# The third value group by seven block products of half its columns, and another order for the last two rows of output tiles

## The chip, the cores and the metric

The kernel runs on one core of one Trainium2 chip. The metric is the device time of one execution in microseconds (us), the median of several runs. A core has five engines that work beside each other, each through its own queue in order: TensorE (PE in the rows; its weight loads are PEld), VectorE (DVE), ScalarE (ACT), GpSimd (POOL) and SyncE (SP), which issues transfers. ACT issues transfers too, in its own queue; those rows carry the name ACTq, as SP's carry SPq.

## The reference, cut to what matters

The kernel is one block of an encoder: a normalised input, one wide projection, three mixers, gates, an output projection and a normalised residual. The change touches the projection of the values of the dilated attention, and the last lines.

```python
h = rms_norm(x, g_pre[layer])                       # 1024 tokens x 1024
a_qkv, bq, ... = jnp.split(h @ w_in[layer], split_at, axis=-1)
a_qkv = a_qkv.reshape(b, s, 3, n_groups * A_HEADS, HEAD_DIM)
av = a_qkv[:, :, 2]                                 # values: three groups of 8 heads x 64 = 512 columns
...
out = merged @ w_out[layer]
x = x + rms_norm(out, g_post[layer])                # 1024 rows, the last tiles of 128 rows end the kernel
```

So one group of values is a product of 1024 tokens by 1024 (contracted) by 512 columns.

## The kernel before

All operands of the big products are kept as a sum of two fp32r parts, high and low. A product of two such operands takes three passes on TensorE: high by high, low by high, high by low. `split` (L104) makes the parts: ACT copies the source into the high part (L105), then DVE subtracts it from the source into the low part (L106).

The values are computed with the tokens as the stationary operand (128 by 128) and the weights as the moving one. Two of the three groups are done together by a block scheme with seven products in place of eight (`PRODUCTS`, L889: A11 by B11, A12 by B21, S2 by T2, S3 by T3, S4 by B22, S1 by T1, A22 by T4). The A and S are blocks of the weights and their sums, the B blocks of the tokens, and the T differences of token blocks that lie in DRAM (`tsd`) in fp32. Each product contracts 512 rows (4 steps k) and gives 512 tokens (4 tiles j) by 512 columns, so a step is 4 x 3 = 12 matmuls, and this first part has 28 steps. The third group (`VG[0]`) then goes the plain way: 2 halves of the tokens by 8 steps k by 4 tiles by 3 passes, 192 matmuls of 512 columns. Both are one loop over `steps_v` (L1088 to L1148), whose matmuls are L1101.

From L886 on the order on ACT, DVE, POOL and SP is the order in which the code is written (`manual_schedule`); TensorE's is so throughout. In each step of the loop the code writes the matmuls first, then the reading of one finished PSUM bank (`left`, `v_evac` L960), then the splits for the step two later (`split_at` L922), sums of weights (`sum_at` L942), the scaled copies with their transfers to DRAM (`v_store` L947: an ACT copy and a transfer that ACT issues), the loads of token differences (`blocks_at` L913), and `operand` (L978), an unrelated job for a later stage in eight rounds of three parts: loads, two DVE instructions, a store. Between the plain steps of the third group it also loads and splits the token differences again, for the keys (`kt_load`, `kt_split`, L1002 and L1006), and prepares the first weights of the keys (`k_load`, `k_sum`, `k_own`). The keys follow (L1165 on): six groups of seven products of 12 matmuls of 512 columns, whose matmuls are in `passes` (L125). Their first product needs the two parts that `k_own(0)` makes.

At the end the output projection runs as seven products too (`z_prod`, L2010). Its last bank, of row tile 7, is done in two halves of 256 columns (L2102 to L2114): each half is added up, squared on ACT with a sum, and weighed; `row(6)` (L2003), which adds row tile 6 to the input and sends it out, stands between the two halves.

Of the kernel before, what the change touches and what calls it, by code (L numbers as in the profile page):

```python
# [8 lines left out]
F32 = mybir.dt.float32  # L9
# [6 lines left out]
S = 1024  # L16
# [34 lines left out]
def block(ctx: ExitStack, tc: tile.TileContext, x, xT, memT, cst, msk, bcst, tabA, gpost,  # L51
# [832 lines left out]

    phase_psum("ps_v", s1=6)
# [4 lines left out]
    SB, TB_, v_rest = {}, {}, {}  # L890
    for k, t in enumerate(ready.pop(len(queue))):
        SB[0, k] = t
    vpp, vp = pool("vp")
    vbp, vb = pool("vb")
# [115 lines left out]
    kt_all = [(nm, k) for nm in ("T2", "T3", "T1", "T4") for k in range(4)]  # L1010
# [79 lines left out]
    for n, (i, e, k) in enumerate(steps_v):  # L1090
        if k == 0:
            now = v_banks()
        for j in range(4):
            if i is None:
                t = slice(e * 512 + j * 128, e * 512 + j * 128 + 128)
                (bh, bl), w, end = (hh[k][:, t], hl[k][:, t]), v_rest[k][0], 7
            else:
                (bh, bl), w, end = tokens_at(i, k, j), SB[i, k], 3
            wh_, wl_ = parts_of(w)
            for q, (a, b) in enumerate(((bh, wh_), (bl, wh_), (bh, wl_))):  # L1100
                PE.matmul(now[j], a, b, start=k == 0 and q == 0, stop=k == end and q == 2)  # L1101
        behind = left.pop(0)() if left else []
        m = n + 2
        if m < CLASSIC:
            split_at(*divmod(m, 4))
        elif m < CLASSIC + 8:
            split(*parts_of(v_rest[m - CLASSIC][0]), v_rest[m - CLASSIC][1])
# [5 lines left out]
        m = n + 5  # L1113
        if m < CLASSIC:
            blocks_at(*divmod(m, 4))
        elif m < CLASSIC + 8 and m % 2 == 0:
            raw = wp.tile([P, 1024], F32, name="wr", bufs=WR)
            nc.sync.dma_start(raw.rearrange("p (k f) -> p k f", k=2), wv[VG[0], :, m - CLASSIC:m - CLASSIC + 2])
            for z in range(2):
                v_rest[m - CLASSIC + z] = (wslot(z) if m < CLASSIC + 4 else slot(), raw[:, half[z]])  # L1120
# [4 lines left out]
        if n == CLASSIC + 4:  # L1125
            close(vbp)
            tpp, tp = pool("tp", "right")
            SF = [tp.tile([P, 512], F32, name=f"sf{j}") for j in range(4)]
        m = n - CLASSIC - 4
        if m >= 0:  # L1130
            for z in kt_all[2 * m:2 * m + 2] if m < 4 else kt_all[m + 4:m + 5]:
                kt_load(*z)
            for z in kt_all[2 * m - 6:2 * m - 4] if 3 <= m < 7 else kt_all[m + 1:m + 2] if 7 <= m < 11 else ():
                kt_split(*z)
            if m == 6:
                k_load(0, 0)
                k_load(0, 1)
            elif m == 10:
                k_own(0)
            elif m == 11:  # L1140
                k_sum(0, 1)
                k_sum(0, 2)
        if k == end:
            for j in range(4):
                if i is None:
                    left.append(lambda b=now[j], T=4 * e + j: [lambda: v_store(vr(), VG[0], T, b)])
                else:
                    left.append(lambda i=i, j=j, b=now[j]: v_evac(i, j, b))  # L1148
# [5 lines left out]
    close(vpp)  # L1154
# [10 lines left out]
    for n in range(6):  # L1165
        for i, (an, bn) in enumerate(PRODUCTS):
# [34 lines left out]
            if n == 0 and i < 4:  # L1201
                kt_split(*kt_all[12 + i])
# [800 lines left out]
    def row(T):  # L2003
# [241 lines left out]
```

## Time and profile before

| | us |
|---|---|
| median of 3 runs (1418.89 to 1419.91) | 1419.02 |
| the profiled execution | 1420.1 |
| its span, first to last instruction | 1418.3 |
| PE busy in the span | 1393.4 (98%) |
| DVE busy | 1040.7 (73%) |
| ACT busy | 670.6 (47%) |
| POOL busy | 505.1 (36%) |

A row of a timeline gives the start, the duration, the engine, the line, the operation, the tile that is written and those that are read, and, in brackets, how long the engine stood idle before it and what released it. "x24" means several alike in a row. A row of a table by stage gives the stretch, its length, the busy time of PE, PEld, DVE, ACT and POOL with the count of instructions, the clock that was granted to TensorE as a share of the full one, the share of the DMA engines' time, and GB/s. The profiled execution took 1.8 us more than its span, and 1.1 us more than the median.

### The profile page before, as it was taken

Reading aid. Unit: us, or ns where it says so; the run is one execution under the profiler, and the core shown is the slowest. Engines: PE = TensorE matmul, PEld = TensorE weight load, DVE = VectorE, ACT = ScalarE, POOL = GpSimd, SP = SyncE. Lnnn points to the kernel's source line nnn. Section 1 sums busy time; section 2 is a strip of 40 time slices with the busy share of each in tenths; the row PEclk is TensorE's granted clock in tenths of the full one; section 3 lists DMA queues with packets and bytes.
Section 4 is the critical chain, followed back from the end, with each engine's and each line's share of the span. In section 5 each row is a group of like instructions: output and inputs, shape, how many; then the busy total and the mean of one; then the engine's idle time right before and its main releaser. Section 6 shows DMA issues by size and latency. Waiting matters only on the chain.

```text
span 1418.3 us, 21284 instructions
## 1 busy us (share of the span) xinstructions
PE 1393.4 (98%) x7496; PEld 1120.2 (79%) x7496; DVE 1040.7 (73%) x1830; ACT 670.6 (47%) x1425; POOL 505.1 (36%) x390
## 2 busy tenths in 40 slices
PE   7999999999999999999999999999999999999997
PEld 7899986656666888888888878787888888888886
DVE  7768677767773695688885777765888788677977
ACT  6544365665555445322146676656543434222232
POOL 0416703766666000432153353520433331034303
PEclk9999999999999999999999999999999999999999
DMA  6356532322210779544543554555353543856255
GB/s 238 108 166 220 182 119 71 112 82 79 75 57 23 260 225 298 162 166 178 193 131 106 129 162 116 140 140 182 106 150 126 178 171 124 321 217 212 93 199 178
DMA packets 122059, 219.67 MB, mean 155 GB/s; under 512 B 25504, under 2 KB 56032, under 8 KB 121952
## 3 DMA queue, kind: packets, MB, share of 16 engines
q1 hardware_dynamic: 95744, 187.60, 41.1%
q10 hardware_dynamic: 26208, 30.71, 6.1%
q8 instruction: 59, 0.97, 0.3%
q14 instruction: 48, 0.39, 0.1%
HBM read 152.88 MB, written 65.37 MB: 154 GB/s over the span
## 4 chain that ended last, share of the span: by engine, by line
PE 78%; DVE 6%; DMA 5%; ACT 5%; issue 3%; POOL 2%; SPq 1%; DVEq 0%; POOLq 0%; ACTq 0%
PE s L125 23%; PE sc L125 9%; PE d L143 6%; PE d L145 6%; PE d L147 6%; PE ov L803 4%; PE s L2019 3%; PE s L1101 3%; PE s L1385 2%; PE tr L1441 2%; PE s L788 2%; PE s L787 2%; PE tr L769 2%; DMA vrt<-rld 2%; PE d L544 2%
## 5 line engine op out<-in xcount | busy, mean ns | idle before, releaser
L143 PE MATMUL d<-hh,wh 128*128 128x512 f32 x480 | 194.9, 406 | 1.7 <-DVE fth L228 1.7
L145 PE MATMUL d<-hl,wh 128*128 128x512 f32 x480 | 194.1, 404 | 0.0
L147 PE MATMUL d<-hh,wl 128*128 128x512 f32 x480 | 190.7, 397 | 0.0
L794 POOL TENSOR_TENSOR bl<-bl,bp 128x512 f32<-128x512 f32 x96 | 130.7, 1362 | 54.4 <-ACT bp L790 49.0
L105 ACT ACTIVATE wh<-wr 128x512 fp32r<-128x512 f32 (+1 forms) x91 | 69.6, 772 | 133.0 <-PE sc L125 78.7
L125 PE MATMUL sc<-hh,wh 128*128 128x512 f32 x384 | 118.4, 389 | 0.0
L106 DVE TENSOR_TENSOR wl<-wr,wh 128x512 fp32r<-128x512 f32 (+1 forms) x63 | 78.9, 1265 | 50.6 <-ACT wh L105 50.6
L143 PEld LDWEIGHTS d<-hh,wh 128*128 128x128 f32 x480 | 90.3, 188 | 27.1 <-issue 6.3
L147 PEld LDWEIGHTS d<-hh,wl 128*128 128x128 f32 x480 | 90.5, 189 | 21.1 <-issue 4.7
L1398 ACT ACTIVATE pra<-pra,sts 128x192 f32<-128x192 f32 (+2 forms) x192 | 84.3, 442 | 47.9 <-DVE sts L1397 47.4
L145 PEld LDWEIGHTS d<-hl,wh 128*128 128x128 f32 x480 | 90.5, 189 | 19.2 <-issue 4.7
L790 ACT ACTIVATE bp<-s 128x512 f32<-128x512 f32 x128 | 75.7, 595 | 43.3 <-PE s L788 42.3
L770 DVE TENSOR_REDUCE bn<-tr 128x1 f32<-128x512 f32 x128 | 84.8, 683 | 12.7 <-PE tr L769 11.3
L106 DVE TENSOR_TENSOR ch<-sf,ch 128x512 fp32r<-128x512 f32 x68 | 55.9, 823 | 40.5 <-ACT ch L105 40.4
L125 PEld LDWEIGHTS sc<-hh,wh 128*128 128x128 f32 x384 | 72.1, 188 | 15.1
L105 ACT ACTIVATE ch<-sf 128x512 fp32r<-128x512 f32 x68 | 41.6, 628 | 89.3 <-PE s L125 46.4
L1249 DVE SCALAR_TENSOR_TENSOR t2a<-d,tab 32x512 f32<-32x512 f32 x96 | 66.0, 687 | 22.4 <-PE d L147 20.7
L1925 POOL TENSOR_TENSOR acc<-acc,th 128x1024 f32<-128x1024 f32 x15 | 41.3, 2756 | 109.9 <-DVE th L1924 109.9
L1039 POOL TENSOR_TENSOR sf<-wr 128x512 f32<-128x512 f32 x12 | 19.0, 1580 | 168.7 <-DMA wr<-in_wu 111.1
L1708 POOL TENSOR_TENSOR sf<-wr 128x512 f32<-128x512 f32 x22 | 28.8, 1329 | 130.4 <-DVE ch L106 81.7
L125 PE MATMUL sc<-hl,wh 128*128 128x512 f32 x192 | 74.7, 389 | 0.0
L1253 POOL TENSOR_TENSOR aq<-t1a,t2a 128x512 f32<-128x512 f32 x24 | 44.5, 1858 | 82.1 <-DVE t1a L1252 82.1
(444 smaller groups left out, 3773.9 us busy)
## 6 DMA issues: line engine op xcount, KB each, us to landing
wr<-in_wu SPq DMA_DIRECT2D x64, 512.0 KB
kd<-kr ACTq DMA_DIRECT2D x48, 256.0 KB
th<-thd SPq DMA_DIRECT2D x24, 512.0 KB
thd<-rs ACTq DMA_DIRECT2D x44, 256.0 KB
g2d<-fth SPq DMA_DIRECT2D x24, 256.0 KB
wos<-os SPq DMA_DIRECT2D x12, 512.0 KB
kraw<-kd SPq DMA_DIRECT2D x12, 512.0 KB
kswp<-kd SPq DMA_DIRECT2D x48, 128.0 KB
```

The lines of the kernel that those rows point to most:

```text
L105: A.activation(dst_h, src, AF.Copy)
L106: V.tensor_tensor(dst_l, src, dst_h.bitcast(F32), op=OP.subtract)
L125: PE.matmul(out_ps, a, b, start=i == 0, stop=i == n - 1)
L143: PE.matmul(dst, wh[:, k, :], hh[k][:, t], start=k == 0, stop=False)
L145: PE.matmul(dst, wh[:, k, :], hl[k][:, t], start=False, stop=False)
L147: PE.matmul(dst, wl[:, k, :], hh[k][:, t], start=False, stop=k == 7)
L770: fp["last"] = V.tensor_reduce(st[i]["n"][:, j, c:c + 1], s, axis=AX.X, op=OP.min)
L790: A.activation(pp, s, AF.Exp, scale=-1.0)
L794: G.tensor_tensor(lsum[i % 2], lsum[i % 2], pp, op=OP.add)
L803: PE.matmul(o[e * 64:e * 64 + 64], VS[:, kt, kv], d.pop(kt), start=kt < 2, stop=kt >= NT - 2)
L1249: V.scalar_tensor_tensor(t2[i], p[j], -0.125, tab[1][j, t], op0=OP.mult, op1=OP.mult)
L1398: A.activation(src, src, AF.Exp, scale=-1.0, bias=bias, accum_out=sts[:, h, 1, T:T + 1])
```

## The change

The first part of the loop keeps its 28 steps; `operand` starts two steps earlier in it, and four transfers of weights for the third group are issued in its step 16. The third group then is a second loop of 28 steps over the same seven products, with half of its 512 columns as the one block and half as the other: a step is 12 matmuls of 256 columns (L1207), two token tiles share a PSUM bank, and the token differences T2, T3, T1, T4 are loaded and split within this loop and kept for the keys. What ACT, DVE, POOL and SP do beside each step is a table (`SIDE`). In the keys the four splits of T4 are gone. The pools `vb` and `vp` change places, since `vp` is closed first now.

The third group's results are scaled and stored by `v3_out`: per bank two ACT copies of 256 columns, each with a transfer of its own.

```diff
-    CLASSIC = 28
-    steps_v = [(i, 0, k) for i in range(7) for k in range(4)] + [(None, e, k) for e in range(2) for k in range(8)]
+    def v3_sum(nm, a, b, op, t=None):
+        V3[nm] = V3[a] if t is None else t
+        V.tensor_tensor(V3[nm], V3[a], V3[b], op=op)
+
+    def v3_split(nm):
+        h, l = wslot(0), wslot(1)
+        split(h, l, V3[nm])
...
+    def v3_out(u, t, b, r):
+        for z in range(2):
+            T = 4 * t + 2 * b + z
+            x = r[:, half_cols[z]]
+            A.activation(x, x, AF.Copy, scale=rcol[:, T:T + 1])
+            nc.scalar.dma_start(vdr[VG[0], 2 * u:2 * u + 2, T * 128:T * 128 + 128].rearrange("p t f -> t p f"),
+                                x.rearrange("t (p f) -> t p f", p=2))
...
+        if nm == "A11":
+            return [lambda: A.activation(v3v[b], ps_, AF.Copy)]
+        if nm == "A12":
+            r = add(r3(), v3v[b])
+            return [lambda: v3_out(0, 0, b, r)]
+        if nm == "S1":
+            x, y = add(r3(), v3y[b]), add(v3v[b], v3v[b])
+            return [lambda: v3_out(1, 1, b, x), lambda: v3_out(0, 1, b, y)]
+        if nm == "A22":
+            y = add(v3y[b], v3y[b])
+            return [lambda: v3_out(1, 0, b, y)]
+        add((v3y if nm == "S3" else v3v)[b], v3v[b])
...
         for stage in (2, 1, 0):
-            r, at = divmod(n - 6 - (0, 2, 3)[stage], 3)
+            r, at = divmod(n - 4 - (0, 2, 3)[stage], 3)
             if at == 0 and 0 <= r < 8:
                 operand(r, stage)
...
+        elif n == 24:
+            v3_split("A11")
+        elif n == 25:
+            v3_sum("S3", "A11", "A21", OP.subtract, V3["A21"])
+        elif n == 26:
+            v3_split("A12")
...
+    SIDE = {0: [lambda: operand(7, 2)], 2: [second], 3: [lambda: [kt_load("T3", k) for k in range(4)]], 4: [lambda: v3_split("S2")],
+            5: more(("T2", 0)), 6: more(("T2", 1), ("T2", 2)),
...
+            9: [lambda: v3_split("S3"), lambda: v3_sum("S4", "A12", "S2", OP.subtract)],
+            10: more(("T3", 0)) + [lambda: [kt_load("T4", k) for k in range(4)]],
+            11: more(("T3", 1)), 12: more(("T3", 2)) + [lambda: k_load(0, 0)], 13: more(("T3", 3)) + [lambda: v3_split("S4")],
...
+            24: more(("T4", 3)), 25: [lambda: k_own(0)], 26: [lambda: k_sum(0, 1)], 27: [lambda: k_sum(0, 2)]}
+    for n in range(28):
...
+        for _ in range(2 if n < 2 else 1):
+            for f in left.pop(0)() if left else []:
+                f()
...
+        for f in SIDE.get(n, ()):
+            f()
...
-            if n == 0 and i < 4:
-                kt_split(*kt_all[12 + i])
...
-        if h == 0:
-            row(6)
+        if h:
+            row(6, (lo,))
+        else:
+            V.tensor_tensor(c11[3][:, e], vs[3][:, e], gp[:, e], op=OP.mult)
         V.scalar_tensor_tensor(r, q[:, 2 * h:2 * h + 1], 1.0 / D, r, op0=OP.mult, op1=OP.add)
-        V.tensor_tensor(c11[3][:, e], vs[3][:, e], gp[:, e], op=OP.mult)
+    V.tensor_tensor(c11[3][:, e], vs[3][:, e], gp[:, e], op=OP.mult)
+    row(6, (hi,))
```

Three places show what this makes of the queues. The first is ACT in the changed kernel, where the third of the seven products runs and the fourth is prepared: r3 are the sums of the second product, vdr the values in DRAM, wh the high part of S3, and kT3 the token differences T3.

```order
L105 ACTIVATE kT23_5727<-kT23_5727 128x512
L1108 ACTIVATE r3_5843<-r3_5843,rcol_79 128x256
L1109 DMA vdr_110<-r3_5843 128x2x128
L1108 ACTIVATE r3_5843<-r3_5843,rcol_79 128x256
L1109 DMA vdr_110<-r3_5843 128x2x128
L1108 ACTIVATE r3_5861<-r3_5861,rcol_79 128x256
L1109 DMA vdr_110<-r3_5861 128x2x128
L1108 ACTIVATE r3_5861<-r3_5861,rcol_79 128x256
L1109 DMA vdr_110<-r3_5861 128x2x128
L105 ACTIVATE wh_5867<-wr_5382 128x1024
L105 ACTIVATE kT30_5743<-kT30_5743 128x512
```

The split of S3 stands behind four scaled copies with four transfers; nothing of this was there before.

The second place is ACT ahead of the keys. In the kernel before, wh is what `k_own(0)` makes for the first key product, and the four stores behind it are those of the last plain half:

```order
L105 ACTIVATE kT12_5874<-kT12_5874 128x512
L105 ACTIVATE kT13_5899<-kT13_5899 128x512
L105 ACTIVATE wh_5951<-wr_5880 128x1024
L948 ACTIVATE vr_5971<-s1_5813,rcol_79 128x512
L949 DMA vdr_110<-vr_5971 128x4x128
L948 ACTIVATE vr_5974<-s1_5814,rcol_79 128x512
L949 DMA vdr_110<-vr_5974 128x4x128
```

In the changed kernel, from the last split of T4 on, with v3v1 a sum that is stored in place:

```order
L105 ACTIVATE kT43_5892<-kT43_5892 128x512
L1108 ACTIVATE r3_6138<-r3_6138,rcol_79 128x256
L1109 DMA vdr_110<-r3_6138 128x2x128
L1108 ACTIVATE r3_6138<-r3_6138,rcol_79 128x256
L1109 DMA vdr_110<-r3_6138 128x2x128
L1108 ACTIVATE v3v1_5716<-v3v1_5716,rcol_79 128x256
L1109 DMA vdr_110<-v3v1_5716 128x2x128
L1108 ACTIVATE v3v1_5716<-v3v1_5716,rcol_79 128x256
L1109 DMA vdr_110<-v3v1_5716 128x2x128
L105 ACTIVATE wh_6149<-wr_5925 128x1024
```

`k_own(0)` has moved behind these four stores, and four like them (r3 and v3v0) stand ahead of the split of T4.

The third place is DVE at the end of the program, where cv3 and cp3 belong to row tile 7, fss7 is its sum of squares, and xt with fss6 is row tile 6. Before:

```order
L2105 TENSOR_TENSOR cv3_12946<-s1_13496,cv3_12946 128x256
L2007 SCALAR_TENSOR_TENSOR xt_13380<-cp2_12941,fss6_12960,xt_13380 128x512
L2007 SCALAR_TENSOR_TENSOR xt_13380<-acc2_12155,fss6_12960,xt_13380 128x512
L2109 SCALAR_TENSOR_TENSOR fss7_12961<-fss7_12961 128x1
L2110 TENSOR_TENSOR cp3_12942<-cv3_12946,rb_78 128x256
L2105 TENSOR_TENSOR cv3_12946<-s1_13496,cv3_12946 128x256
L2109 SCALAR_TENSOR_TENSOR fss7_12961<-fss7_12961 128x1
```

And in the changed kernel:

```order
L2179 TENSOR_TENSOR cv3_13144<-s1_13694,cv3_13144 128x256
L2184 TENSOR_TENSOR cp3_13140<-cv3_13144,rb_78 128x256
L2185 SCALAR_TENSOR_TENSOR fss7_13159<-fss7_13159 128x1
L2179 TENSOR_TENSOR cv3_13144<-s1_13694,cv3_13144 128x256
L2080 SCALAR_TENSOR_TENSOR xt_13578<-cp2_13139,fss6_13158,xt_13578 128x512
L2185 SCALAR_TENSOR_TENSOR fss7_13159<-fss7_13159 128x1
L2186 TENSOR_TENSOR cp3_13140<-cv3_13144,rb_78 128x256
L2080 SCALAR_TENSOR_TENSOR xt_13578<-acc2_12353,fss6_13158,xt_13578 128x512
```

The second half of row tile 7 is summed ahead of both halves of row tile 6, whose halves leave as two transfers in place of one.

More of the change, by code (lines that the diff above doesn't have):

```diff
@@ L1008, in kt_split @@
         split(h, l, l.bitcast(F32))
-    kt_all = [(nm, k) for nm in ("T2", "T3", "T1", "T4") for k in range(4)]
     KR = {}
@@ L1112, in block @@
             f()
[L1113 to L1120, printed above, removed]
+        if n < 23:
+            blocks_at(*divmod(n + 5, 4))
@@ L1126, in block @@
             close(vbp)
+            v3p, v3 = pool("v3")
             tpp, tp = pool("tp", "right")
+            v3v, v3y = [[v3.tile([P, 512], F32, name=f"v3{x}{b}") for b in range(2)] for x in "vy"]
+        elif n == 5:
             SF = [tp.tile([P, 512], F32, name=f"sf{j}") for j in range(4)]
[L1129 to L1148, printed above, removed]
+        for f in SIDE.get(n, ()):
+            f()
+        if k == 3:
+            left += [lambda i=i, b=b, z=now[b]: v3_evac(i, b, z) for b in range(2)]
     while left:
@@ L1153, in block @@
             g()
-    close(vpp)
+    close(v3p)
     tbp, tb = pool("tb")
```

78 lines of the change are left out of this document (59 added, 19 removed).

## The prediction

> **What bounds the kernel now.** I read the page first, for the span and the chain that ended last, then the table by stage around the value groups, then the timelines of PE, ACT and DVE there and at the end.
>
> ```profile
> span 1418.3 us, 21284 instructions
> PE 1393.4 (98%) x7496; PEld 1120.2 (79%) x7496; DVE 1040.7 (73%) x1830; ACT 670.6 (47%) x1425; POOL 505.1 (36%) x390
> PE 78%; DVE 6%; DMA 5%; ACT 5%; issue 3%; POOL 2%; SPq 1%; DVEq 0%; POOLq 0%; ACTq 0%
> ```
>
> ```profile
> 483.00:538.00 55.00, 54.66 (x240) 44.63 (x239) 50.56 (x83) 26.99 (x45) 0.00 (x0) 1.00 0.73 229
> 538.00:582.00 44.00, 43.43 (x192) 35.61 (x192) 21.24 (x28) 18.79 (x31) 7.62 (x5) 1.00 0.86 280
> ```
>
> The span is a string of matmuls, so a us of PE work saved is a us of time as long as nothing else comes late. The two stages differ in the other engines, though. In the block products (483 to 538) DVE is busy for 50.56 of 55 us; in the plain third group (538 to 582) DVE and ACT are busy for half the time. The change turns the second kind of stage into the first kind.
>
> **The change: PE work.** The plain group runs from its first matmul to the first one of the keys:
>
> ```profile
> 538.04 0.39 PE L1101 MATMUL s<-wh,hh 128*128 128x512 f32 x1
> 582.42 0.39 PE L125 MATMUL s<-hh,wh 128*128 128x512 f32 x1
> ```
>
> That is 44.38 us for 192 matmuls of 512 columns. The new loop has 28 x 12 = 336 of 256 columns. An unbroken run of such a shape stands early in the trace, 24 rows one behind the other:
>
> ```profile
> 99.07 0.28 PE L311 MATMUL d<-wbh,hh 128*128 128x256 f32 x1
> 101.78 0.28 PE L315 MATMUL d<-wbl,hh 128*128 128x256 f32 x1
> ```
>
> 23 distances in 2.71 us are 0.118 each, so 336 take 39.6 us: **4.8 us less**, if PE never waits. A step of 12 is 1.41 us, a product 5.65. [...]
>
> **The queues beside it.** The prices come from these rows:
>
> ```profile
> 541.17 0.71 ACT L948 ACTIVATE vy<-vy,rcol 128x512 f32<-128x512 f32 x1
> 541.91 0.37 ACTq L949 DMA_DIRECT2D vdr<-vy  x1
> 542.32 0.63 ACT L105 ACTIVATE wl<-wr 128x512 fp32r<-128x512 f32 x1 [0.44 <-ACT vy L948]
> L401 ACT ACTIVATE mh<-mt,cs 128x256 fp32r<-128x256 f32 x8 | 3.4, 499 | 0.0
> 591.39 0.62 ACT L105 ACTIVATE kT<-kT 128x512 fp32r<-128x512 f32 x1
> 591.91 1.05 ACT L105 ACTIVATE wh<-wr 128x1024 fp32r<-128x1024 f32 x1
> 592.86 0.62 ACT L105 ACTIVATE kT<-kT 128x512 fp32r<-128x512 f32 x1
> 514.42 0.68 DVE L106 TENSOR_TENSOR wl<-wl 128x512 fp32r<-128x512 f32 x1
> 515.03 0.68 DVE L972 TENSOR_TENSOR vy<-d,vv 128x512 f32<-128x512 f32 x1
> L518 DVE TENSOR_TENSOR wl<-wr,wh 128x1024 fp32r<-128x1024 f32 x8 | 9.8, 1223 | 1.5 <-ACT wh L517 1.4
> ```
>
> ACT: a copy of 512 columns 0.53 from start to start, of 1024 columns 0.96, a store (copy and transfer) of 512 columns 1.15, because the transfer holds the queue for 0.44 behind the copy. No store of 256 columns is in the trace: between 0.50 (the scaled copy of L401 alone) and 1.15 I take 0.94, that copy plus the same 0.44. DVE: 512 columns 0.60, 1024 columns 1.15 (1.22 less the same overlap). From one engine to the next I add 0.07.
>
> With these I walk the queues in their written order. t is the time from the start of step 24 of the first loop, whose last four steps take 4 x 2.72 = 10.9; there PE begins the new loop. At t = 0 I take DVE and ACT to be on time, as the rows of before around 527 show DVE coming out of a round of `operand` there (1.33 for its two instructions):
>
> ```profile
> 526.51 0.68 DVE L988 SCALAR_TENSOR_TENSOR vot<-vot,vgt 128x512 f32<-128x512 f32 x1
> 527.84 0.68 DVE L957 TENSOR_TENSOR vr<-s,vy 128x512 f32<-128x512 f32 x1
> ```
>
> **Wait 1, ahead of S2 x T2.** Up to the split of S2, DVE has 12 bank sums (7.2), two block splits with their token parts (2.4), two rounds of `operand` (2.7), the low parts of A11 and A12 and the sums S3 and S2 (4.6): 16.9 of work. ACT has 12 stores (13.8), four copies (2.1), two of 1024 (1.9), one bank copy (0.5): 18.3. They also wait for each other: the copy of A12 stands behind the third pair of stores, which wait for sums that DVE makes behind S3, so it ends at 13.2; DVE's part of A12 ends at 14.4, the last bank sums at 19.3, S2 at 20.5; the four stores of those sums end at 22.2, S2's copy at 23.7, its low part at 24.9, and the low part of T2's first tile, which the second matmul reads, at 25.5. PE gets there at t = 10.9 + 11.3 = 22.2. **PE waits 3.3.**
>
> **Wait 2, ahead of S3 x T3.** From 25.5 DVE splits three more tiles of T2 (27.3), then sums the second product's banks; ACT's four stores of them run from 28.0 to 31.7, S3's copy ends at 32.7, its low part at 33.9, the sum S4, written ahead of the tokens, at 35.05, and T3's first low part at 35.65. PE ended S2 x T2 at 31.2. **PE waits 4.5.** Without any lag from wait 1 the same chain, 3.8 + 0.96 + 1.15 + 1.15 + 0.6 behind the end of the second product, would be 7.6 against the product's 5.65: still 2.
>
> The next three products fit: S4's low part is there at 39.8 for 41.4, S1's at 44.5 for 47.0.
>
> **Wait 3, the last product and the keys.** S1 x T1 ends at 52.7. DVE's two sums of its first bank are done at 53.2, ACT's four stores at 56.45, the last T4 copy at 57.0, its low part at 57.65; PE wanted it at 56.9: 0.8. Only then DVE sums the second bank; its four stores end at 62.1, `k_own`'s copy at 63.0, its low part at 64.3. PE has finished A22 x T4 at 59.1. The first two key matmuls go at 63.1, the third at 64.3: **4.8**. Before, this split was done long ahead (ACT at 570, DVE at 573, for 582.42):
>
> ```profile
> 570.34 1.05 ACT L105 ACTIVATE wh<-wr 128x1024 fp32r<-128x1024 f32 x1
> 572.76 2.31 DVE L106 TENSOR_TENSOR wl<-wr,wh 128x1024 fp32r<-128x1024 f32 x1
> ```
>
> Four more stores then delay the block S2 of the keys by 0.6 against the third key product. Waits: 3.3 + 4.5 + 0.8 + 4.8 + 0.6 = **14.0**. The store's price is what moves this most: with 0.50 for 256 columns the same walk gives 8.2, with 1.15 it gives 17.5. The four T4 splits that leave the keys save nothing, as PE did not wait there. The loads of T2 are issued when the last `operand` store is out (17.0) and are wanted at 24: hidden, with some 3 us to spare behind the landing.
>
> **First loop.** `operand` now comes two steps earlier:
>
> ```profile
> 477.41 1.51 SPq L985 DMA_DIRECT2D vrt<-rld  x2
> 478.45 7.30 DMA vrt<-rld
> 488.24 0.68 DVE L988 SCALAR_TENSOR_TENSOR vot<-vot,vgt 128x512 f32<-128x512 f32 x1
> ```
>
> Its loads move up by only two transfers' issue, about 0.9, so they land near 484.9 instead of 485.75, while DVE wants them at about 483.3 (488.24 less two steps' share of its queue), ahead of the splits for step 9, which PE reaches at 460.94 + 9 x 2.72 = 485.4. DVE then ends them near 486.7. The stage had 0.9 of waiting (538.04 - 460.94 less 336 distances of 0.2267); I take 1.1 more, between 0 and 3.
>
> ```profile
> 460.94 0.39 PE L1101 MATMUL s<-wh,hh 128*128 128x512 f32 x1
> ```
>
> **The end.**
>
> ```profile
> 1409.53 0.42 DVE L2105 TENSOR_TENSOR cv<-s,cv 128x256 f32<-128x256 f32 x1
> 1410.12 0.75 DVE L2007 SCALAR_TENSOR_TENSOR xt<-cp,fss,xt 128x512 f32<-128x512 f32 x1 [0.17 <-POOL fss L130]
> 1411.85 0.42 DVE L2105 TENSOR_TENSOR cv<-s,cv 128x256 f32<-128x256 f32 x1
> 1413.84 0.75 DVE L2113 SCALAR_TENSOR_TENSOR xt<-acc,fss,xt 128x512 f32<-128x512 f32 x1 [0.44 <-POOL fss L2111]
> ```
>
> The second half's sum waits for row(6), two instructions of 0.66, from 1410.12. Without them it starts near 1410.7, and the last two instructions, with row(6)'s second half now just ahead of them, near 1412.8: 1.0 less. Against it, row(6)'s second transfer leaves 1.3 later and shares the DMA engines with the last two; 0 to 1.0, I take 0.8.
>
> **Sum.** -4.8 + 14.0 + 1.1 - 0.8 = +9.5. The profiled execution (1420.1, of which 1.8 lie around the span) becomes 1429.6; it stood 1.1 above the median, so the median becomes **1428.5**.
>
> **Rivals.**
> *A slow clock behind a wait.* After its last matmul at the end, PE kept the full clock until 1413.0, 3.5 us later, and had half of it then; at the start, matmuls of 256 columns stand 0.21 apart for 3.7 us before they reach 0.12.
>
> ```profile
> 1403.74 5.75 PE L2019 MATMUL s<-hh,hl 128*128 128x512 f32 x36
> 1412.50:1413.00 0.50, 0.00 (x0) 0.00 (x0) 0.10 (x2) 0.37 (x2) 0.00 (x0) 1.00 0.97 401
> 1413.00:1413.50 0.50, 0.00 (x0) 0.00 (x0) 0.40 (x2) 0.00 (x0) 0.36 (x1) 0.51 0.97 401
> 8.03 0.41 PE L381 MATMUL s<-wbh,hl 128*128 128x256 f32 x1
> 8.24 0.41 PE L381 MATMUL s<-wbl,hh 128*128 128x256 f32 x1
> ```
>
> Waits 2 and 3 have 4.5 and 4.0 without steady work. If they count, each costs 3.7 x (1 - 0.118/0.21) = 1.6: 1430.1 or 1431.7. Against it: each gap holds a lone matmul or two, and neither is far over 3.5. [...]
>
> *The stores' issue does not hold ACT.* If every store cost its copy alone (0.50 and 0.72), the walk leaves 4.8 of waiting: -4.8 + 4.8 + 1.1 - 0.8, 1419.3, no change. The 0.44 in the row at 542.32 speaks against it.
>
> *Faster: DVE and ACT keep up throughout.* PE alone would then set the stage, -4.8 - 0.8: 1413.4. It needs the chain behind the second and the sixth product to fit in 5.65 in place of 7.6 and 11.4, so stores of 256 columns would have to cost under about 0.2. No row is that short.
>
> *More waiting than walked:* POOL's sums for the keys run beside `k_own`, as at 572.76, where 1024 columns took 2.31, and a transfer may be late: up to 1437.
>
> **Chances.** Forecast 0.55, one or two slow stretches 0.20, no change 0.08, faster 0.10, more waiting 0.07. The range takes in the store's two ends (14.0 becoming 8.2 or 17.5, so 1422.7 to 1432.0), the first loop's, the slow stretches and, below, the case of no change: **1418 to 1436**. Faster by over 0.2% (2.8 us, about what a measurement of this kernel can tell from no change) 0.10, within 0.08, slower 0.82.
>
> **What would show it.** In the profile after: PE idle of 3 to 5 us at the start of the third and the fourth product and at the first key matmul, released by DVE's kT and wl of L106; ACT without a pause through the stores; the granted clock of those stretches; matmuls of 256 columns 0.118 apart; the last transfer about 1 us closer to PE's last matmul. I am wrong if PE runs through the new loop in 40 to 43 us, or if the stores take ACT less than 0.8.

## The result, and the profile after

The changed kernel takes **1441.31 us** (median of 5 runs, 1440.89 to 1442.77), beside 1419.91 for the kernel before on the same chip: a ratio of 1.0153, interval 1.0138 to 1.0167. That is 21.4 us slower, where the forecast was 9.5. Its profiled execution took 1442.0, with a span of 1440.2; that of before, 1420.1 and 1418.3. So the spans differ by 21.9, and this is the sum that is taken apart here.

The page of the changed kernel:

```profile
span 1440.2 us, 21632 instructions
PE 1400.0 (97%) x7640; PEld 1129.7 (78%) x7640; DVE 1052.9 (73%) x1847; ACT 677.4 (47%) x1434; POOL 504.1 (35%) x390
```

PE is busy for 6.6 us more, although it was given 4.8 us less to do. Matmuls of 256 columns stand 0.21 apart where the clock was a half (568.96 to 569.18) and 0.12 where it was full, so a busy PE says little here. The table by stage says more (stretch, its length, busy time of PE, PEld, DVE, ACT and POOL, granted clock, share of the DMA engines, GB/s). The stretches are the first loop, the first five and the last two products of the new loop with the first keys, and 35 us of the keys:

```profile
461.00:541.90 80.90, 77.71 (x337) 62.51 (x336) 61.68 (x98) 33.92 (x57) 0.00 (x0) 1.00 0.82 263
541.90:582.00 40.10, 32.09 (x242) 31.01 (x241) 25.97 (x35) 20.25 (x31) 0.00 (x0) 0.91 0.68 217
582.00:605.50 23.50, 17.80 (x114) 15.59 (x113) 10.10 (x14) 9.91 (x17) 5.05 (x4) 0.85 0.35 106
605.50:640.00 34.50, 34.03 (x146) 27.07 (x145) 24.90 (x32) 9.50 (x15) 15.77 (x9) 1.00 0.41 142
```

The loss is in three rows: PE stands idle for 3.2 of the first loop, for 8.0 and 5.7 in the two pieces of the new one, and there the clock was 0.91 and 0.85. PE's own rows show where (in brackets: idle before, and what ended it):

```profile
541.80 0.28 PE L1207 MATMUL s<-wh,hh 128*128 128x256 f32 x1
...
548.81 0.36 PE L1207 MATMUL s<-wh,hh 128*128 128x256 f32 x1 [1.10 <-DVE vy L958]
...
555.98 0.39 PE L1207 MATMUL s<-wh,kT 128*128 128x256 f32 x1 [1.18 <-ACT kT L105]
556.83 0.39 PE L1207 MATMUL s<-wh,kT 128*128 128x256 f32 x1 [0.47 <-DVE kT L106]
...
562.46 0.28 PE L1207 MATMUL s<-wl,kT 128*128 128x256 f32 x1
566.11 0.58 PE L1207 MATMUL s<-wh,kT 128*128 128x256 f32 x1 [3.37 <-ACT kT L105]
568.58 0.58 PE L1207 MATMUL s<-wh,kT 128*128 128x256 f32 x1 [1.90 <-DVE kT L106]
568.96 0.42 PE L1207 MATMUL s<-wl,kT 128*128 128x256 f32 x1
...
592.37 0.38 PE L1207 MATMUL s<-wh,kT 128*128 128x256 f32 x1 [0.29 <-ACT kT L105]
593.93 0.39 PE L1207 MATMUL s<-wh,kT 128*128 128x256 f32 x1 [1.18 <-DVE kT L106]
...
599.70 0.80 PE L125 MATMUL s<-hh,wh 128*128 128x512 f32 x1 [4.20 <-ACT wh L105]
```

These are the waits that were walked, at the places that were named, and one more (548.81: the second product's bank is one that DVE has yet to read for the first loop's last product). From one start to the next, less the 0.1194 of an undisturbed matmul here, they are 1.3, 2.1, 6.1, 1.9 and 4.4: 15.7 in a loop of 57.9. Behind the third and the last, matmuls stand 0.21 (568.96) and 0.42 (512 columns) apart. ACT's queue at the two large ones reads as it was written:

```profile
560.61 0.51 ACT L1108 ACTIVATE r<-r,rcol 128x256 f32<-128x256 f32 x1 [1.36 <-DVE r L1119]
561.15 0.37 ACTq L1109 DMA_DIRECT2D vdr<-r  x1
561.56 0.51 ACT L1108 ACTIVATE r<-r,rcol 128x256 f32<-128x256 f32 x1 [0.44 <-ACT r L1108]
...
564.48 1.06 ACT L105 ACTIVATE wh<-wr 128x1024 fp32r<-128x1024 f32 x1 [0.44 <-ACT r L1108]
```

A store of 256 columns takes 0.95 from start to start (0.94 was the price), and the split of S3 begins 3.9 behind the first of four. The clock, us by us, around that wait (the granted clock is the third number from the end):

```profile
565.00:566.00 1.00, 0.00 (x0) 0.00 (x0) 0.43 (x1) 1.00 (x3) 0.00 (x0) 1.00 1.08 382
566.00:567.00 1.00, 0.58 (x1) 0.29 (x1) 1.00 (x2) 1.00 (x3) 0.00 (x0) 0.56 1.10 365
...
572.00:573.00 1.00, 1.00 (x7) 1.00 (x7) 1.00 (x2) 0.00 (x0) 0.00 (x0) 0.53 1.02 369
573.00:574.00 1.00, 1.00 (x11) 1.00 (x10) 1.00 (x3) 0.00 (x0) 0.00 (x0) 1.00 1.06 401
```

It falls to a half near 566.1 and comes back near 572.9, 6.8 later. In the first loop, SP's queue shows what was not walked at all, with ACT and PE behind it:

```profile
512.11 0.51 SPq L1093 DMA_DIRECT2D wr<-in_wv  x1
512.74 3.67 SPq L921 DMA_DIRECT2D sl<-tsd  x3
...
521.96 4.49 SPq L921 DMA_DIRECT2D sl<-tsd  x3
```

```profile
521.91 0.63 ACT L105 ACTIVATE sl<-sl 128x512 fp32r<-128x512 f32 x1 [12.14 <-DMA sl<-tsd]
```

```profile
522.59 0.49 PE L1148 MATMUL s<-sl 128*128 128x512 f32 x1 [1.11 <-ACT sl L105]
```

Three loads of token differences are issued right behind the four transfers of step 16 (the last at 512.11), and that takes SP 3.7 us. The kernel before needs 1.5 for the like:

```profile
515.93 1.47 SPq L920 DMA_DIRECT2D sl<-tsd  x3
```

Then SP stands 0.9, 1.2 and 1.0 in the next round of `operand`, until three of the four transfers have landed, and so comes to the next three loads at 521.96. (2.9 of the 4.5 there is something else: the third load waits until PE has read the old contents of its tile.) ACT gets the first of these loads at 521.91, 9.2 after SP began to issue it, and PE waits for ACT.

The spans add up from PE's first matmul of each stage: start -0.2; first loop 81.1 for 77.1, +4.0; the new loop up to the first key matmul 57.9 for 44.4, +13.5; from there to the third key product 7.63 for 5.44, +2.2 (the slow clock, and a wait that e5_filler separates from it); to the first matmul of the attention +1.0; from there to the last product +2.4; the end -1.0. Together 21.9.

One caution belongs to the first of these. Its loop is the same program in the kernel before and in e1_tail and e14_tail5 below, and took 77.1, 76.2 and 76.2 in their traces. So a difference under 1 us in this loop says little, and the 4.0 could as well be 4.9. The plain third group took 43.6 to 44.4 in these three.

### The profile page after: what moved, and what is told of

Its sections match the earlier page's. It is cut to its first block, busy times and chain, and to the rows that moved or that the text cites. A ratio compares the mean times of both kernels' runs of the same rounds, so it can differ in the third digit from the quotient of the medians.

```text
span 1440.2 us, 21632 instructions
## 1 busy us (share of the span) xinstructions
PE 1400.0 (97%) x7640; PEld 1129.7 (78%) x7640; DVE 1052.9 (73%) x1847; ACT 677.4 (47%) x1434; POOL 504.1 (35%) x390
## 4 chain that ended last, share of the span: by engine, by line
PE 72%; DVE 8%; ACT 6%; DMA 5%; POOL 3%; issue 3%; SPq 1%; ACTq 1%; DVEq 0%; POOLq 0%
PE s L125 21%; PE sc L125 9%; PE d L143 6%; PE d L145 5%; PE d L147 5%; PE s L2093 4%; PE ov L803 3%; PE s L1458 2%; PE s L788 2%; PE s L787 2%; PE tr L1514 2%; PE tr L769 2%; PE d L544 2%; PE d L2093 2%; PE s L1207 1%
## 5 line engine op out<-in xcount | busy, mean ns | idle before, releaser
L106 DVE TENSOR_TENSOR wl<-wr,wh 128x1024 fp32r<-128x1024 f32 (+1 forms) x65 | 81.5, 1265 | 61.9 <-ACT wh L105 61.9
L1326 POOL TENSOR_TENSOR aq<-t1a,t2a 128x512 f32<-128x512 f32 x24 | 48.5, 2023 | 82.3 <-DVE t1a L1325 82.3
```

Of the source, the lines that this page charges most:

```text
L106: V.tensor_tensor(dst_l, src, dst_h.bitcast(F32), op=OP.subtract)
```

## The experiments

Ratios are to the kernel before, timed beside each on the same chip; its medians were 1418.9 to 1419.5. "The changed kernel" stands at 1.0153. A difference "of ratio" is the difference of two ratios times 1419.

**e3_sp: are ACT's stores the wait?**

```diff
-            nc.scalar.dma_start(vdr[VG[0], 2 * u:2 * u + 2, ...
+            nc.sync.dma_start(vdr[VG[0], 2 * u:2 * u + 2, ...
```

> The changed kernel with the third group's stores issued by SP instead of ACT: the same 24 scaled copies on ACT, no transfer in its queue. Theory: a transfer holds ACT for 0.44 behind its copy, so four stores cost 3.8 in front of the split of S3 and in front of k_own; with the copies alone (0.5 each) they cost 2.0. Wait 2 (5.9 us in the trace) falls by about 1.8 to 4, the last two (1.8 and 4.3) to about 1 and 2.5, and the two stretches of slow clock (2 us each) go with them where a gap stays under 3.4 us: 6 to 9 us less than the changed kernel, 1432 to 1435. Rival: the wait is set by the chain of sums and copies, not by the issue: 0 to 2 us less. Second rival: SP, which now waits for ACT's copies, holds the loads of T1, T4 and of the keys' first weights behind it, and as much is lost there: 1441 or more.

1435.17, ratio 1.0107 (1.0086 to 1.0128): 6.5 us of ratio less. ACT's row at the place of the four stores:

```profile
560.32 1.71 ACT L1108 ACTIVATE r<-r,rcol 128x256 f32<-128x256 f32 x4 [1.36 <-DVE r L1119]
561.93 1.04 ACT L105 ACTIVATE wh<-wr 128x1024 fp32r<-128x1024 f32 x1
```

Four copies take 1.6 instead of 3.9, PE's idle time there is one of 2.1, the one in the last product is gone and the last is 1.3. The loads behind SP's stores cost nothing there. The theory holds for the waits, and the rivals fall. The slow clock did not go, though the theory had it go: two stretches of 6.8 became three of 3.4. One of these, 566.8 to 570.2, stands behind the idle time of 2.1 (563.9 to 566.0), so a gap under 3.4 us, which the theory had as safe, was not safe here (the gap at 566.11 in the changed kernel was 3.37).

**e7_defer: or the order alone?** The stores stay on ACT, but those of the second product are written six steps later.

```diff
+                if 8 <= n < 12:
+                    late.append(f)
+                else:
+                    f()
...
+        if n in (14, 15):
+            late.pop(0)()
```

> The changed kernel with the four stores of the second product (still issued by ACT) written behind steps 14 and 15 instead of 8 and 9, so that nothing stands ahead of the split of S3. Theory: wait 2 is the queue of ACT alone; S3's copy then ends near 560.4 instead of 565.5, its low part near 562.4, S4's sum 563.5, T3's first low part 564.2, for PE at 562.6: wait 2 falls from 5.9 to 1.5 and the slow clock behind it (2.0) goes, so 6 to 6.5 less: 1434.5 to 1435.5. Rival: DVE's own sums in that stretch or the loads of T3 are next in line at about the same time: 2 us less or nothing.

1436.16, ratio 1.0118 (1.0101 to 1.0135): 5.0 us of ratio less, where 6 to 6.5 were expected. Wait 2 is down to 1.2, under the 1.5 that was expected, and no slow matmul follows it:

```profile
564.45 0.39 PE L1208 MATMUL s<-wh,kT 128*128 128x256 f32 x1 [1.16 <-DVE kT L106]
```

The loop is 51.2 long for 57.9, so this place alone was worth 6.7 in the trace.

**e4_kown: the same question ahead of the keys.**

```diff
-23: more(("T4", 2)),
-            24: more(("T4", 3)), 25: [lambda: k_own(0)],
+23: more(("T4", 2), ("T4", 3)) + [lambda: k_own(0)],
```

> The changed kernel with the last split of T4 and k_own(0) written two steps earlier, ahead of the eight stores of the sixth product. Theory: the 1.8 of waiting in the last product and the 4.3 ahead of the keys, with the slow clock behind it (about 1.9), come only from those stores standing first in ACT's queue: all three go (8 us), and about 4 come back at the keys' third product, because its block S2 still stands behind twelve stores: 3 to 5 us less than the changed kernel, 1436 to 1438. Rival: k_own's copy waits for its slot until the sixth product is done and holds the stores, whose sums then hold up PSUM banks: no gain, 1440 to 1443.

1440.25, ratio 1.0148 (1.0133 to 1.0163), hardly better. The loop is 51.1 long, and all its late waits are gone, but the keys' third product then waits for its block S2 behind twelve stores:

```profile
603.27 7.13 PE L125 MATMUL s<-kT,ch 128*128 128x512 f32 x24 [4.89 <-ACT ch L105]
```

A wait of 4.4 became one of 4.9 with a slow clock behind it: the 24 matmuls stand 0.29 apart on the mean (603.27 to 610.23), where 512 columns are 0.23 apart at the full clock. The mechanism was as expected, the gain given back almost whole; 3 to 5 less was too hopeful.

**e5_filler: does the slow clock come from the idle time?** Matmuls are added whose results nothing uses.

```diff
+        if n == 12:
+            for _ in range(44):
+                PE.matmul(now[0][:, half_cols[0]], hh[0][:, :128], hh[0][:, :256], start=True, stop=True)
...
+            if (n, i) == (0, 0):
+                for _ in range(16):
+                    PE.matmul(dst, hh[0][:, :128], hh[0][:, lo], start=True, stop=True)
```

> The changed kernel with matmuls added that compute nothing which is used: 44 of 256 columns (44 x 0.118 = 5.2 us) on PE ahead of the product S3 x T3, where PE waits 5.9 us, and 16 of 512 columns (3.6 us) ahead of the first key matmul, where it waits 4.2 to 4.4. Theory: TensorE falls to half its clock when it stood nearly idle for over 3 us, and that is why the trace shows 256-column matmuls 0.21 apart from 568.6 to 573.0 and 512-column ones 0.42 apart from 599.7 to 603.7 (some 2 us each). With PE kept at work it keeps its clock, and the kernel gets 3 to 4 us FASTER by 60 more matmuls: 1437.5 to 1438.5. Rival: the clock falls for another reason (load, a fixed time) or the fillers make the real matmuls later: 1441 or more, with the slow rows still there.

1438.35, ratio 1.0136 (1.0121 to 1.0151): 2.4 us of ratio faster by 60 matmuls more, 3.4 in the spans. The two intervals overlap, so the clock has to decide: its four runs had a mean of 0.997 to 0.999, the five of the changed kernel 0.992 to 0.994. In its trace:

```profile
core 0: 1436.8 us, clock 0.999
```

The loop with its fillers takes 55.8 for 57.9, the first two key products 6.4 for 7.6: 2.1 and 1.2 less. The slow clock is shown, and the idle time as its cause; the theory's "over 3 us" fits the gaps of 3.37 and 4.20 filled here, not the shorter ones in other runs (2.1 in e3_sp, 2.3 in e12_loads_alone). The first two key products still take 0.9 more than the 5.4 of before, at the full clock: there the third matmul waits for `k_own`'s low part.

**e2_spread, e9_early: the four transfers elsewhere.** One each in steps 19 to 22, or in 11 to 14.

```diff
-        if n == 16:
...
+        if 19 <= n < 23:
+            j = (n - 19) // 2
+            if n % 2:
+                v3_load(f"A1{j + 1}", va[:, j * 1024:j * 1024 + 1024])
+            else:
+                v3_load(f"A2{j + 1}", wp.tile([P, 1024], F32, name="wr", bufs=WR))
```

> The changed kernel, its four transfers of 0.5 MB each for the third group issued one each in steps 19 to 22 of the first loop instead of all in step 16. Theory 1: these 2 MB stand ahead of the six loads of token differences that SP issues right behind them (the trace shows those loads held on SP for 3.7 and 4.5 us), and that is what made the first loop 3.8 us longer (80.9 against 77.1): the loop comes back to 77 to 78.5, and the time falls by 2.5 to 3.5 us against the changed kernel, to about 1438. Rival: the loop is longer because operand comes two steps earlier, as the prediction had it; then nothing of the 3.8 goes, 1441. Rival 2: the later loads are now late for the split of A11 in step 24 and the waits move into the second loop: 1440 to 1443.

> The changed kernel with the four transfers issued one each in steps 11 to 14, where the rows of before show the DMA engines least loaded (0.60 of their time from 500 to 510, against 0.81 and more behind that) and no load of token differences is due. Theory: in step 16 they stand ahead of six loads of token differences, in steps 19 to 22 ahead of the last loads of operand, and PE waits for either; in steps 11 to 14 for neither. The first loop then takes 77.5 to 78.5 in place of 81.1, and the time falls by 2.5 to 3.5: 1438 to 1439. Rival: DVE, which is busy without a pause in this stretch, is what makes the end of the loop late, wherever the transfers are: 80 to 81.5 and 1440 to 1442.

1440.23, ratio 1.0144 (1.0129 to 1.0159), and 1439.91, ratio 1.0146 (1.0129 to 1.0163): neither can be told from the changed kernel by its time. The traces say more: the first loop took 78.8 and 77.8, for 81.1. But it is not steady: with steps 19 to 22 two other kernels below had 79.3 and 81.4, with steps 11 to 14 two others 79.5 and 80.2, and five with step 16 had 80.7 to 81.5. Wherever the 2 MB go, something of this stretch stands behind them now and then. In e2_spread it is `operand`: its load of the gates is issued behind three of the four transfers, and DVE stands idle for it for 2.6 until 531.88, with the splits for the last product behind.

**e11_op_alone, e12_loads_alone: each edit of the first loop by itself,** in the kernel before.

```diff
-            r, at = divmod(n - 6 - (0, 2, 3)[stage], 3)
+            r, at = divmod(n - 4 - (0, 2, 3)[stage], 3)
```

> The kernel before with operand two steps earlier in the first loop, and nothing else. The prediction gave this edit 1.1 us (0 to 3). Theory now: it costs 0.3 to 0.8 (small waits near 495 and 503 that all kernels with the edit show) and saves the two rounds that stand in the plain group: 1418.5 to 1420, no difference that can be told. Rival, the prediction's own step: 1.1 or more, 1420 to 1422.

```diff
+        if n == 16:
+            va = vb.tile([P, 4, 512], F32, name="vA11").rearrange("p a b -> p (a b)")
+            for j in range(2):
+                for u, t in ((0, va[:, j * 1024:j * 1024 + 1024]), (1, wp.tile([P, 1024], F32, name="wr", bufs=WR))):
+                    nc.sync.dma_start(t.rearrange("p (k f) -> p k f", k=4), wv[VG[0], :, 4 * j:4 * j + 4, 256 * u:256 * u + 256])
```

> The kernel before with the four transfers of 0.5 MB added in step 16 of the first loop; nothing reads what they bring. Theory: six loads of token differences stand behind 2 MB, and PE waits for their splits near 522 and 530: the first loop grows by 1.5 to 3, the time to 1420.5 to 1422. Rival: without the splits of A11 and A12 in steps 24 to 26 DVE makes up for it, and nothing is lost: 1419 to 1420.

`operand` alone: 1420.63, ratio 1.0011 (1.0002 to 1.0021), its first loop 78.0 (460.67 to 538.67), 0.9 longer than in the trace of before and 1.8 longer than in the traces of e1_tail and e14_tail5, which leave this loop as it was. The forecast's 1.1 fits both the time and the trace, and my new theory of "no difference" was too low. But PE does not wait at 485.4, where the forecast had it: the largest delay is 0.6 at 494.47. The transfers alone: 1423.88, ratio 1.0033 (1.0021 to 1.0044), 4.7 us of ratio, more than I expected; the first loop 80.2 (460.58 to 540.82), 3.1 longer. What PE waited for is the split of a token difference, and DVE had itself stood idle just ahead of it for a load of `operand`, which is also issued behind the transfers:

```profile
525.82 2.50 PE L1101 MATMUL s<-sl 128*128 128x512 f32 x5 [2.28 <-DVE sl L106]
```

```profile
522.06 0.69 DVE L988 SCALAR_TENSOR_TENSOR vot<-vot,vgt 128x512 f32<-128x512 f32 x1 [2.15 <-DMA vgt<-g2d]
```

The clock was a half from 525.6 until 529, 3.4 long, which makes 1.6 of the 3.1; in the changed kernel's first loop it stayed at 1.00. So 0.9 and 3.1 make up the 4.0 there only in size. In the changed kernel the waits near 522 and 523 are the transfers' (from start to start 1.8 more than undisturbed); the wait at 539.17 may be due to what DVE is given in steps 24 to 26.

**e6_operand: both undone in the changed kernel.** e2_spread, with `operand` back at its old place and its last round in steps 0 and 1 of the second loop.

```diff
-    SIDE = {0: [lambda: operand(7, 2)], 2:
+    SIDE = {1: [lambda: operand(7, 1), lambda: operand(7, 2)], 2:
```

> The kernel of e2_spread (four weight transfers in steps 19 to 22) with operand back at its old place, two steps later in the first loop. Together the two undo all that the change did to the first 24 steps. Theory: of the 3.8 us by which the first loop grew, the transfers made 2.3 and operand the rest (1.1 was forecast): the loop takes 77 to 78 us instead of 78.8, against 77.1 before. The last two rounds' instructions then fall into the second loop, ahead of S2's sum on DVE: wait 1 may grow by up to 1.3. In all 1438.5 to 1440. Rival: the first loop stays at 78.8, because it is the four splits and sums of steps 24 to 26 on DVE that make its end late (the 1.5 us wait at the last product), and operand does not matter: 1440 to 1442.

1438.57, ratio 1.0138 (1.0123 to 1.0153), first loop 79.3. The time is the theory's, but not by its way. In this loop the rival is nearer: the last product still waits 2.1 for DVE, even where `operand` is at its old place. DVE's rows ahead of that wait show both other causes: 2.2 of idle time for loads of `operand` that stand behind the transfers, and 1.7 for ACT's copy of A11, which step 24 added. This run can't weigh the two. The time came down in the attention instead, which is 2.8 shorter than in e2_spread.

**e13_both: do the pieces add up?** e9_early and e5_filler in one kernel.

> The changed kernel with two pieces of its loss undone at once: the four transfers in steps 11 to 14 (as in e9_early) and the matmuls that only keep PE at work ahead of S3 x T3 and ahead of the keys (as in e5_filler). Theory: the 12 us between forecast and result are these two (3.3 and 3 to 4) and a rest of 5 in small waits that the walk of the queues left out; the two don't touch each other, so the time is 1441.4 - 3.3 - 3.2, about 1435. Rival: what one gives back the other hides (a loop that ends sooner waits longer at the next late operand): 1437.5 to 1439.

1436.05, ratio 1.0118 (1.0103 to 1.0134), clock 0.999, span 1434.8: 5.3 under the changed kernel in the spans, 5.0 by the ratios, where 6.5 was expected. Its first loop was 79.5, not 77.8; the rest adds up.

**e8_combo, e10_best: all remedies.** e8_combo: transfers in steps 19 to 22, stores on SP, `k_own` as in e4_kown, and

```diff
-            9: [lambda: v3_split("S3"), lambda: v3_sum("S4", "A12", "S2", OP.subtract)],
-            10: more(("T3", 0)) + [lambda: [kt_load("T4", k) for k in range(4)]],
...
+            8: [lambda: v3_split("S3")], 9: more(("T3", 0)) + [lambda: v3_sum("S4", "A12", "S2", OP.subtract)],
+            10: more(("T3", 1)) + [lambda: [kt_load("T4", k) for k in range(4)]],
...
+        if n in (10, 11):
+            late.pop(0)()
```

> All remedies in one: the four transfers in steps 19 to 22, the stores issued by SP, the split of S3 in step 8 and T3's splits from step 9 with the second product's stores behind steps 10 and 11, the sum S4 behind T3's first split, the last split of T4 and k_own ahead of the sixth product's stores. Theory: what stays is 1.1 (the bank that waits for vy), 2.0 (wait 1), about 1 at the keys' block S2, and 1.7 of the first loop; no slow clock. Against before: +1.7 - 4.3 + 3.1 + 1.0 - 1.0 at the end, and some 1 to 2 of small waits later: 1419 to 1422, no change against before. Rival: SP's queue holds loads behind the stores, so T1, T4 or the keys' weights are late: 1424 to 1430. Better than before only if DVE's gaps at the end of the first loop close too.

1430.35, ratio 1.0079 (1.0064 to 1.0094): 8 over the theory, by the rival's way, and with e10_best the best of the block scheme, still 11 slower than before. The new loop now takes 42.7, less than the plain group's 43.6 to 44.4. What is left lies on both sides of it:

```profile
538.11 4.38 PE L1148 MATMUL s<-sl 128*128 128x512 f32 x11 [2.41 <-DVE sl L106]
...
613.19 7.04 PE L125 MATMUL s<-kT,ch 128*128 128x512 f32 x22 [3.18 <-ACT ch L105]
```

Ahead of it the first loop waits 2.4 and then runs 11 matmuls in 4.2 instead of 2.5, with the clock a half from 538.5 to 541.9. Behind it the keys' second group waits 3.2 for its weights, with slow matmuls after it (22 in 7.0, 0.32 each, for 0.23 at the full clock): SP issues their load only when the stores and the tables are out, ACT waits 5.5 for it and then 5.2 for POOL's sum, and from the third key product to the attention it takes 138.2 for 133.1.

```profile
588.65 2.04 SPq L1109 DMA_DIRECT2D vdr<-v3y  x4
590.80 1.80 SPq L1244 DMA_DIRECT2D tab<-in_tabA  x2
592.65 22.17 SPq L1016 DMA_DIRECT2D wr<-in_wu  x4
```

e10_best moves the last stores to GpSimd's queue and the transfers to steps 11 to 14:

```diff
+            (nc.sync if (u, t) == (0, 0) else nc.gpsimd).dma_start(vdr[VG[0], 2 * u:2 * u + 2, ...
...
+ [lambda: k_own(0)] + [lambda j=j: k_sum(0, j) for j in (1, 2, 3, 4)]}
```

> The kernel of e8_combo, with the transfers in steps 11 to 14 as in e9_early, the stores of the sixth and seventh product issued by GpSimd instead of SP, and the four sums for the keys' first group in step 23. Theory: the first loop gives 3 back, and the tables and the keys' second weights no longer wait on SP behind eight stores, so the 3.2 of waiting at the keys' second group goes with its slow clock (2): 1423 to 1426. It is faster than before (under 1416) only if wait 1 and the bank that waits for vy go too, which nothing here touches. Rival: GpSimd's own issue of a transfer is slow or holds its sums, and the keys' block S2 is late: 1428 to 1435.

1431.59, ratio 1.0078 (1.0061 to 1.0095), no better, by the rival's way: GpSimd takes 0.72 for each transfer, and the tables start later still, since their pool takes the place of the third group's, which is still being stored:

```profile
593.05 2.89 POOL L1109 DMA_DIRECT2D vdr<-v3y  x4
```

```profile
594.68 5.24 SPq L1243 DMA_DIRECT2D tab<-in_tabA  x2
```

The keys' second group then waits 5.8.

**e1_tail, e14_tail5: the end alone,** the last hunk of the change with `row`, in the kernel before.

> The kernel before with the new order at the end alone (second half of row tile 7 summed ahead of row tile 6, two transfers for row tile 6); the value group stays plain. Theory: the end saves the 0.8 to 1.0 us that the walk of DVE's last instructions gave, so the time is 1.0 below the kernel before, and the whole of the 21.4 lost lies in the value group and behind it. Rival: the end saves nothing or loses (row(6)'s second transfer shares the DMA engines with the last two): within 0.3 of before, and the lower distance from PE's last matmul to the end in the changed kernel would be chance.

> The kernel of e1_tail again, with more rounds: its interval (0.9984 to 1.0003) left open whether the new order at the end alone is faster than the kernel before. Theory: 0.8 to 1.1 us faster (its trace and that of the changed kernel both end 1.0 sooner behind PE's last matmul), a ratio of 0.9992 to 0.9995. Rival: no difference, 0.9998 to 1.0002.

1418.11, ratio 0.9994 (0.9984 to 1.0003), and with more rounds 1417.76, ratio 0.9993 (0.9985 to 1.0002). Both say some 1 us less, neither interval leaves out no difference. The traces are clearer: from the start of PE's last matmul to the end of the span it is 9.1 before and 9.1 and 9.2 in e11_op_alone and e12_loads_alone, whose end is unchanged, but 8.0 in e1_tail and in e14_tail5 and 8.1 in the changed kernel. The last transfer's issue ends 6.2 behind PE's last matmul before, and 5.1 in the changed kernel. Before:

```profile
1415.29 0.37 ACTq L2114 DMA_DIRECT2D out<-xt  x1
```

In the changed kernel:

```profile
1426.59 5.75 PE L2093 MATMUL s<-hh,hl 128*128 128x512 f32 x36
```

```profile
1437.08 0.37 ACTq L2191 DMA_DIRECT2D out<-xt  x1
```

This half of the change is the only part that I would keep.

## Why the prediction was wrong

The direction and the main mechanism were right; the sum was 12.4 short. Point by point:

- **PE work, -4.8.** 336 matmuls at 0.1194 are 40.1: -4.3. Right but for 0.5.
- **Waits 1 to 3, 14.0.** Measured 2.1 for 3.3, 6.1 for 4.5, 1.9 for 0.8, 4.4 for 4.8, and nothing for 0.6 at the keys' first block S2: 14.5. With the bank that waits for `vy` (1.3), which the walk left out by taking PSUM banks as free, 15.7, 1.7 of the miss. The 0.07 from one engine to the next was an estimate of mine; in the rows of before DVE starts 0.67 behind ACT's start of a copy of 512 columns (540.63 and 541.30), where the walk has 0.53 and 0.07, 0.60. The price of a store was right (0.95); e3_sp and e7_defer show the mechanism.
- **The slow clock, a rival with 0.20.** It came twice. The sum of the spans leaves 2.1 for it in the loop and 2.2 at the keys, 4.3 of the miss; e5_filler gives back 2.1 and 1.2 of these, and the 0.9 that it leaves at the keys is a wait for `k_own`'s low part, so that the wait at the keys, 4.8 in the forecast, was rather 5.3 than 4.4. The step that failed is "Against it: each gap holds a lone matmul or two, and neither is far over 3.5". The lone matmul at 566.11 did not keep the clock, which stayed a half to 572.9, and a gap need not be over 3.5: it was 3.37 there, and 2.3 in e12_loads_alone. It belonged in the sum, since the forecast's own waits brought it about.
- **First loop, 1.1.** The `operand` part was right in size (0.9 in e11_op_alone, 1.8 against the shorter traces of the same loop), though not in place. The four transfers of step 16, which the section on the change names, have no price anywhere in the prediction. Alone they cost 3.1 in the trace of e12_loads_alone and 3.0 to 6.2 by its timed runs. This step failed by leaving something out: the transfers that the change adds were not walked through SP's queue, where six loads stood behind them. So did the loads of `operand`. 2.9 of the miss, with a part of the splits in steps 24 to 26 that the runs don't separate (e6_operand).
- **Behind the keys, nothing.** The trace has 1.0 up to the attention (0.6 of it a wait for a block of the keys' second group) and 2.4 in it, for which the prediction had no term: 3.4 more. Of the 2.4, the rows of PE's waits show 1.3. One of them, with DVE and POOL ahead of it, in the changed kernel:

```profile
843.31 1.48 DVE L106 TENSOR_TENSOR wl<-wr,wh 128x512 fp32r<-128x512 f32 x1 [0.20 <-ACT wh L105]
```

```profile
842.78 3.13 POOL L1389 TENSOR_TENSOR ak<-kraw,kswp 128x512 f32<-128x512 f32 x2 [4.56 <-DMA std<-sr]
```

and in the kernel before, the same instructions:

```profile
821.46 0.69 DVE L106 TENSOR_TENSOR wl<-wr,wh 128x512 fp32r<-128x512 f32 x1 [0.20 <-ACT wh L105]
```

```profile
821.95 4.36 POOL L1316 TENSOR_TENSOR ak<-kraw,kswp 128x512 f32<-128x512 f32 x2 [5.59 <-DMA std<-sr]
```

  Before, POOL began 0.5 behind DVE's start, and DVE took 0.69; now it begins 0.5 ahead, and DVE takes 1.48. PE then waits 0.38 at 845.12 and 0.84 at 850.94, where it waited nothing and 0.15 before. A second such meeting, at 906.39 (POOL 0.35 ahead, DVE 1.48), costs nothing: PE waits 0.88 at 914.03, but it waited 0.85 there before too, without one. The rows show the two durations, 0.69 against 1.48, and the order of the starts; why DVE takes longer was not shown. What moved POOL against DVE stays open. The later start of the keys alone does not: in e6_operand they come 17 us later than before, POOL begins 0.2 behind DVE, DVE takes 0.69, and the attention is no longer than before.
- **The end, -0.8.** -1.0 in the spans; about -1 in two timed kernels, neither beyond its interval. Right.

The range failed for one reason more: the slow clock and "more waiting" were set against the forecast as alternatives, each with its own time, while in the kernel they came on top of it and of each other.

## What to carry to other kernels

When a wait of some microseconds is forecast for TensorE, add the slow clock behind it to the sum at once (here 1.6 behind a gap of 2.3 in e12_loads_alone, and the 2.1 and 1.2 that e5_filler gave back behind gaps of 3.4 and 4.2), and ask which transfers the same edit puts in front of which loads. A stage like the plain group, which kept DVE busy for 21.2 and ACT for 18.8 of its 44.0 us, lends the rest to its neighbours: a scheme that saves 10% of TensorE's work there and takes all of that time pays on both sides, as e8_combo shows, whose loop is 0.9 to 1.7 shorter than the plain one and which is 11 slower. Ahead of a long chain on TensorE, write the splits before the stores, and look at what then stands behind the stores: e7_defer kept its gain, e4_kown gave it back.

## What the runs showed of the hardware

The clock of TensorE fell at 566.1 and 596.8 in the changed kernel and came back at 572.9 and 603.7: each stretch is 6.8 long, and 30.7 lie between the two falls. Shorter stretches, of 3.4, are those of e3_sp (566.8 to 570.2), e12_loads_alone (525.6 to 529.0) and e8_combo (538.5 to 541.9). What I had not expected is how little idle time is enough: gaps of 2.1 in e3_sp, of 2.3 in e12_loads_alone and of 2.4 in the first loop of e8_combo, while a gap of 2.1 in e6_operand (536.0 to 538.1) left it at 1.00. Nor is there one length behind which it falls: behind PE's last matmul it stayed full for 3.5 in the kernel before (until 1413.0) and for 4.2 in the changed one (1432.3 to 1436.5). In the 3.4 us ahead of the two falls of the changed kernel PE stood idle for 3.4 and 1.8. So no length of a gap divides the cases here; what does was not shown.

A transfer issued by ACT held that queue for 0.44 behind a copy of 512 columns (542.32 in the kernel before), and for 0.44 to 0.50 behind one of 256 (561.56 to 564.48 in the changed kernel); one issued by GpSimd took 0.72 of its queue (four in 2.89 in e10_best). Scaled copies of 256 columns without transfers ran 0.40 apart (four in 1.61 in e3_sp).
